# A hybrid Mamba and sparse-attention layer on one core: who loads the projection weights, and where the first norm's root is applied

## The chip, the cores and the metric

The kernel runs on one core of a Trainium2 chip. The metric is device time in microseconds, from runs without the profiler; three runs of the kernel before are given below, and the profiled execution has a time of its own. The core has a matrix engine (TensorE, "PE" in the profile; its weight loads are "PEld"), VectorE ("DVE"), ScalarE ("ACT"), GpSimd ("POOL") and SyncE ("SP"). SP issues most of the DMAs here, and POOL issues those that accumulate.

## The reference

One decoder layer on 512 tokens of width 1024, batch 1, in float32:

```
h    = rms_norm(x, norm1_g)
proj = h @ w_in                                  # 1024 x 5184
z, xbc, dt, q, kv, gates = split(proj)
y_ssm = ssd_mixer(z, xbc, dt, ...)               # conv of 4 taps, silu, 16 heads, 4 chunks of 128
y_nsa = rms_norm(nsa_mixer(q, kv, gates, ...), attn_norm_g)
x = x + concat([y_ssm, y_nsa]) @ w_out
h = rms_norm(x, norm2_g)
u = causal_dwconv(h @ ffn_w_up, ...)             # 1024 x 5632, 3 taps
x = x + (silu(ug) * uv) @ ffn_w_down
return rms_norm(x, final_norm_g)
```

`nsa_mixer` gives each query three attentions (over compressed blocks, selected blocks and a window); with 512 tokens all blocks are selected. Rotary embedding is applied to q and to the three kinds of k. The compressed keys and values come from blocks of 32 tokens through a small two-layer network. `rms_norm` divides each token's row by the root of its mean square: the root is one number per token, so it can be applied to `x` ahead of a product, or to the product behind it.

## The kernel before

**Exact products out of three fast ones.** A float32 operand is split into a high part (rounded to the fast format, `F32R`) and a low part (the rest). Each product is made of three matmuls: high by high, high by low, low by high. `hT` holds the two parts of the normed input, transposed: 8 blocks of 128 features by 512 tokens.

**Granules.** All big weights are cut into granules of 128 x 1024 numbers, 512 KB each, numbered in the order of their use: 0 to 39 are `w_in`, 40 to 55 `w_out`, from 56 the feed-forward weights. Of `w_in`, 0 to 3 are the two kinds of plain v, 4 and 5 the keys and 6 and 7 the values that get compressed, 8 and 9 further keys, 10 to 13 queries, 14 and 15 the first of xbc, and so on. Of `w_out`, 40 to 47 take the attention's output and 48 to 55 the SSM's. A granule comes into the chip in one of two ways:

- *split by the engines*: SP loads two halves `wr` of 256 KB, ACT or DVE rounds each to `wh`, and DVE or POOL subtracts to get `wl`;
- *split by loads* (granules `D0` to `D1 - 1`): POOL loads the whole granule to `wh` (the load rounds), ACT writes `-wh` into `wl` (1024 columns), and POOL loads the granule a second time, accumulating onto `wl`.

`wh` and `wl` have `N_WH` and `N_WL` buffers; halves `wr` and nearly all other tiles of 128 x 512 share `N_SLOT` slots. PSUM is a pool of 8 banks.

**Order.** The whole program is recorded first (`record`), with dependencies. Then `schedule` makes a list schedule from a table of costs: at each step it takes the operation that can start first, ties by priority, on five in-order engines, with limited buffers. Operations recorded with `DP` may go to DVE or POOL, plain copies to ACT or DVE. So any change of buffers, costs or operations shifts the order on every engine; the order that comes out is fixed at build time.

**The start** (`first_job`). `N_WARM` matmuls on zeros keep PE busy while the first loads come. Norm 1's root is not known yet, so the v products (`psa`, 96 matmuls) are made from `x` times the norm's gain, in temporary parts `xgh` and `xgl`, and the root is applied in `evac_v`. Beside this the sum of squares is made (`n1ss`), then its root (`n1r`, and `n1rb`: spread over all partitions). Then `hT` is made: per block one multiply by gain and root on DVE (`xT`), one copy to `hTh`, one subtract to `hTl`. After that come the products of granules 4 to 7 (`psb`, 24 matmuls each), and the small projection of dt and gates (`psd`, 16 matmuls).

**Compression.** The keys in `evac_c` are rotated (`rope`: four DMAs `rw` exchange halves, three operations on DVE or POOL), and then each pair is copied by four DMAs into `x2a` and `x2b`; `compress` gathers blocks from these into `cxb` and multiplies (`cps`). SP issues all of these DMAs.

**The middle** weaves attention (units of 128 queries, `pss`, `tb`, `o`) with the other projection granules. Then `ssd` (four chunks) is woven with `out_nsa`, the product of the attention's output with granules 40 to 47, and `out_ssm` follows with granules 48 to 55, four for each half of the columns: all four of a half are held while the four token tiles go by. The feed-forward is last, PE at work without a break.

Of the kernel before, what the change touches and what calls it, by code (L numbers as in the profile page):

```python
# [10 lines left out]
F32 = mybir.dt.float32  # L11
F32R = mybir.dt.float32r
# [7 lines left out]
P = 128  # L20
# [3 lines left out]
KC = 8  # L24
FF = 2816
NEG = -1.0e30
N_SLOT = 53
N_WH = 7
N_WL = 7
AHEAD = 3  # L30
LOOK = 2
D0, D1 = 8, 56
N_EAGER = 3
HEADS = (4, 2, 1, 1)
N_WARM = 10
P_MAX = 8
T_COLD = 6830.0
LAG = 3


# [128 lines left out]
class Program:  # L169
# [82 lines left out]
    def _cost(self, op, e, n, args, kw, ins, outs):  # L252
        is_ps = [v.buf.pool.tag == "b" for v in ins]
        if e == "PE":
            o, l = outs[0], ins[0]
            if l.buf.dt == BF16:
                return max(o.free / 2.4, 53 * l.free / 128) + 2.5, 0

            passes = 2 if l.buf.dt == F32 and n != "transpose" else 1
            cost = passes * max(o.free * passes / 2.4 + 13.3, 110 * l.free / 128)  # L260
            part = l.ids.shape[0]
            return cost + (190 if part <= 64 else 0), 0
        if e == "ACT":
            extra = sum(isinstance(kw.get(x), View) for x in ("scale", "bias", "accum_out"))
            return ins[0].free / 1.2 + (52 if is_ps[0] else 94) + 93 * extra, TABLE.get(args[2].name, 0)
        if n == "dma_start" and e == "POOL":
            v = outs[0]
            op.lat = v.ids.shape[0] * v.free * 4 / (180.0 if "accum_op" in kw else 360.0)
            return 1000.0, 0
        if e in ("DVE", "POOL"):  # L270
            f = max([v.free for v in ins] + [outs[0].free])
            if n == "reciprocal":
                cost = f * 6.25 + 70
            elif n == "memset":
                cost = f / 0.96 + 10
            elif n in ("tensor_scalar", "tensor_scalar_mul", "tensor_scalar_add", "tensor_scalar_max", "tensor_copy"):
                cost = f / (0.96 if is_ps[0] else 1.92) + 68 + 61 * (len(ins) > 1)
            else:
                cost = f / 0.96 + 75 + (61 if n == "scalar_tensor_tensor" and len(ins) > 2 else 0)
            if e == "DVE" and any(int(v.ids.flat[0]) // v.buf.row for v in ins + outs):  # L280

                cost += 97
            if f >= 64:
                big = [v for v in ins if v.free >= 64]
                sb = sum(v.buf.pool.tag != "b" for v in big)
                op.port[e] = e == "POOL" or sb > 1 or (sb == len(big) == 1 and not is_ps[0] and n not in ("reciprocal", "tensor_reduce"))
            return cost * (2.0 if e == "POOL" else 1.0), 0
        v = (outs + ins)[0]
        op.lat = v.ids.shape[0] * v.free * 4 / 360.0
        return 650.0, 0  # L290


# [119 lines left out]
def layer_kernel(ctx: ExitStack, tc: tile.TileContext, x, xt, win, wdtg, wout, wup, wdn, pack, gcol, rows, cw1, consts, rot, out):  # L412
# [17 lines left out]
    def slot(name, dt=F32, shape=(P, T)):  # L430
        return alloc(sp, shape, dt, name, "s", N_SLOT)

    def bank(name, shape=(P, T)):
        return alloc(pp, shape, F32, name, "b", 8)
# [300 lines left out]
    def job_dtg():  # L735
# [12 lines left out]
        raw64 = slot("dtg", F32, (64, T))  # L748
        S.activation(raw64, ps[64:128], AF.Copy)
        V.tensor_add(raw64, raw64, ps[0:64])  # L750
        yield 1.0
        tb = bank("dtgT", (P, NT, 64))
        for t in range(NT):
# [32 lines left out]
    def evac_c(which, pair):  # L786

        def f(ps):
            if which == "k":
                r = rope(ps, 1.0)  # L790
            else:
                r = slot("vcr")
                S.activation(r, ps, AF.Copy)
            x2 = slot("x2a"), slot("x2b")
            for a in range(2):
                own = slice(64 * a, 64 * a + 64)
                SP.dma_start(x2[a][0:64, :], r[own, :])
                SP.dma_start(x2[a][64:128, 0:511], r[own, 1:512])
            CX[which, pair] = x2
        return f  # L800
# [217 lines left out]

    def evac_xbc(i):
        def f(ps):  # L1020
            o = slot("xbc")
            w = [k("cw", 5 * i + j) for j in range(5)]
            S.activation(o, ps, AF.Identity, bias=w[4], scale=w[3])
            for d in range(1, 4):
                V.scalar_tensor_tensor(o[:, d:], ps[:, :T - d], w[3 - d], o[:, d:], op0=ALU.mult, op1=ALU.add)
            XB[i] = o
        return f

# [2 lines left out]
    def evac_z(qr):  # L1031
        def f(t, ps):
            if qr % 2 == 0:
                Z[t, qr // 2] = slot("z")
            S.activation(Z[t, qr // 2][:, (qr % 2) * 256:(qr % 2 + 1) * 256], ps, AF.Copy)
        return f

    SS = {}
# [159 lines left out]
    def nsa_root(h):  # L1198
        ps = bank("oss", (P, 2, 2))
        for t in range(2):  # L1200
            for p_ in range(2):
                mm(ps[:, t], ACC[h][:, p_, t], ones[:, 0:2], start=p_ == 0, stop=p_ == 1)
        r = rstd_of(ps[:, :, 0], 2, 1024, 1e-6, "nsa")
        for t in range(2):
            RS["nsa", 2 * h + t] = r[:, t:t + 1]


    def first_job():

        g0 = nxt(4)
        ps = [bank("psa") for _ in range(NT)]
        acc = slot("n1acc")
        for j in range(KC):
            g = gT[:, j:j + 1]
            xh, xl = slot("xgh", F32R), slot("xgl", F32R)
            S.activation(xh, xT[j], AF.Copy, scale=g)
            V.scalar_tensor_tensor(xl, xT[j], g, xh.bitcast(F32), op0=ALU.mult, op1=ALU.subtract)  # L1220
            if j % 2 == 0:
# [14 lines left out]
            mm(ss[:, t], acc[:, t * P:(t + 1) * P], ones[:, 0:2], start=True, stop=True)  # L1236
        r = rstd_of(ss[:, :, 0], NT, 1, 1e-6, "n1")
        RS["n1"] = r
        rb = bank("n1rb")
        for t in range(NT):  # L1240
            mm(rb[:, t * P:(t + 1) * P], r[:, t:t + 1].to_broadcast([P, P]), ident, start=True, stop=True)
        for j in range(KC):
            V.scalar_tensor_tensor(xT[j], xT[j], gT[:, j:j + 1], rb, op0=ALU.mult, op1=ALU.mult)
            S.activation(hT[0][:, j], xT[j], AF.Copy)
            DP.tensor_sub(hT[1][:, j], xT[j], hT[0][:, j].bitcast(F32))
        pr.first = False
        for t in range(NT):
            for z, ty in enumerate("sw"):
# [134 lines left out]
    def out_nsa(half):  # L1383
        if half == 0:
            for h in range(2):
                for g in range(4):
                    if g >= N_EAGER:
                        nsa_ops(g, h)
                nsa_root(h)
        for t in range(NT):  # L1390
            X1[t, half] = slot(f"xr{t}")
            SP.dma_start(X1[t, half], x[t * P:(t + 1) * P, half * 512:(half + 1) * 512])
        g0 = nxt(4)
        ws = [w_get(g0 + p_, 3 - p_) for p_ in range(4)]
        for t in range(NT):
            ps = bank(f"on{t}")
            for p_ in range(4):
                for j in range(2):
                    tri(ps, mix(t, 2 * p_ + j), [a[:, j * 512:(j + 1) * 512] for a in ws[p_]],
                        p_ == 0 and j == 0, p_ == 3 and j == 1)  # L1400
                yield 1.3
            V.scalar_tensor_tensor(X1[t, half], ps, RS["nsa", t], X1[t, half], op0=ALU.mult, op1=ALU.add)

    def out_ssm(half):
        g0 = nxt(4)
# [205 lines left out]
```

## Time and profile before

| | before |
|---|---|
| median of 3 runs | 919.08 us (918.53 to 921.29) |
| profiled execution, own time | 917.42 us |
| its span, first to last instruction | 915.6 us |
| PE busy | 883.9 us, 97% |
| DVE busy | 682.8 us, 75% |
| ACT busy | 433.0 us, 47% |
| mean granted TensorE clock | 0.994 |

The span is 1.8 us shorter than the profiled execution's own time; what lies outside is start and end. Busy time of PE is the time in which some matmul was in flight, and matmuls overlap, so it says where PE stood idle and not how fast it went. Where engines wait, the profile names what ended the wait.

### The profile page before, as it was taken

To read this page: it belongs to the slowest core of one execution; us is meant where nothing else is said; L and a number is where in the kernel's file an instruction comes from. 1 tells how busy PE (TensorE), PEld (TensorE's weight loads), DVE (VectorE), ACT (ScalarE), POOL (GpSimd) and SP (SyncE) were. 2 spreads that over 40 slices of the span, in tenths; PEclk is the share of its full clock that TensorE was granted. 3 is DMA by queue.
4 is the path that set the end of the run, shared out by engine and by line. 5 is a ranking of instruction groups with operands and counts; after the bars stand their busy time and mean duration, and the time that the engine had idled before them with its cause. 6 is when DMAs were issued, how large, how long until landed. Compare 5 with 4: busy or idle time off the path is not lost.

```text
span 915.6 us, 13236 instructions
## 1 busy us (share of the span) xinstructions
PE 883.9 (97%) x4621; PEld 727.6 (79%) x4621; DVE 682.8 (75%) x1466; ACT 433.0 (47%) x939; POOL 111.0 (12%) x138
## 2 busy tenths in 40 slices
PE   8998999999999999999999999999999999999996
PEld 5776777787887799888777779888888888888885
DVE  6956899998889876689898477777773347777535
ACT  5624577787676666578665244222321113222113
POOL 0331231111111111102322221000000000000000
PEclk9999999999999999999999999999999999999999
DMA  8798754454454454432859922111112661000002
GB/s 274 222 223 204 168 119 96 95 121 106 103 127 93 93 105 103 93 116 48 209 165 304 332 83 93 54 50 47 47 58 98 227 226 35 1 0 1 1 1 92
DMA packets 45217, 106.02 MB, mean 116 GB/s; under 512 B 5984, under 2 KB 6752, under 8 KB 45152
## 3 DMA queue, kind: packets, MB, share of 16 engines
q0 software_dynamic: 13824, 50.34, 24.6%
q1 hardware_dynamic: 31328, 54.86, 18.3%
q8 instruction: 36, 0.59, 0.3%
q14 instruction: 29, 0.24, 0.1%
HBM read 97.31 MB, written 2.10 MB: 109 GB/s over the span
## 4 chain that ended last, share of the span: by engine, by line
PE 74%; DVE 10%; DMA 6%; issue 6%; ACT 2%; POOL 2%; SPq 1%; POOLq 0%; DVEq 0%; ACTq 0%
PE psb L400 36%; PE dn L400 13%; PE psa L400 8%; PE pss L400 5%; PE tb L400 4%; PE o L400 4%; PE os L400 2%; DMA rw<-rx 1%; DMA x2b<-rx 1%; PE on L400 1%; DVE hTl L400 1%; DMA wl<-in_wout_dram 1%; DMA x2b<-vcr 1%; SPq L400 1%; DMA wr<-in_win_dram 1%
## 5 line engine op out<-in xcount | busy, mean ns | idle before, releaser
L400 PE MATMUL psb<-hTh,wh 128*128 128x512 f32 (+1 forms) x600 | 232.8, 390 | 2.5 <-ACT cup L400 1.0
L400 PE MATMUL psb<-hTl,wh 128*128 128x512 f32 (+1 forms) x600 | 230.4, 384 | 2.3 <-DVE hTl L400 2.3
L400 PE MATMUL psb<-hTh,wl 128*128 128x512 f32 (+1 forms) x600 | 230.0, 384 | 0.0
L400 ACT ACTIVATE wh<-wr 128x512 fp32r<-128x512 f32 x80 | 49.8, 631 | 202.0 <-PE psb L400 102.1
L400 PEld LDWEIGHTS psb<-hTh,wh 128*128 128x128 f32 x600 | 113.2, 189 | 23.7 <-ACT cup L400 1.5
L400 PEld LDWEIGHTS psb<-hTl,wh 128*128 128x128 f32 x600 | 113.3, 189 | 23.5 <-DVE hTl L400 3.6
L400 PEld LDWEIGHTS psb<-hTh,wl 128*128 128x128 f32 x600 | 113.2, 189 | 21.6
L400 DVE TENSOR_TENSOR wl<-wr,wh 128x512 fp32r<-128x512 f32 x133 | 90.2, 714 | 17.1 <-ACT wh L400 16.8
L400 DVE CAST wh<-wr 128x512 fp32r<-128x512 f32 x68 | 28.9, 426 | 91.9 <-PE psb L400 43.7
L400 ACT ACTIVATE p<-pss,nm 128x128 f32<-128x128 f32 (+3 forms) x128 | 66.8, 525 | 38.0 <-DVE nm L400 21.3
L400 PE MATMUL dn<-wh,gTh 128*128 128x512 f32 (+1 forms) x186 | 70.3, 378 | 0.0
L400 PE MATMUL dn<-wl,gTh 128*128 128x512 f32 (+1 forms) x186 | 70.3, 378 | 0.0
L400 PE MATMUL dn<-wh,gTl 128*128 128x512 f32 (+1 forms) x186 | 70.2, 378 | 0.0
L400 DVE TENSOR_TENSOR ptl<-tb,pth 128x512 fp32r<-128x512 f32 x80 | 54.3, 687 | 14.6 <-ACT pth L400 11.0
L400 ACT ACTIVATE wl<-wh 128x1024 fp32r<-128x1024 f32 x48 | 50.6, 1056 | 27.7 <-DMA wh<-in_wout_dram 14.9
L400 DVE TENSOR_REDUCE nm<-pss 128x1 f32<-128x384 f32 (+3 forms) x88 | 55.5, 633 | 4.0 <-PE pss L400 3.4
L400 PE MATMUL tb<-ck,p 128*128 128x128 f32 x320 | 51.4, 275 | 1.4 <-DVE p L400 1.0
L400 POOL TENSOR_TENSOR wl<-wr,wh 128x512 fp32r<-128x512 f32 x15 | 21.0, 1410 | 225.6 <-ACT wh L400 206.2
L400 ACT ACTIVATE pth<-tb 128x512 fp32r<-128x512 f32 x62 | 36.9, 598 | 21.9 <-PE tb L400 16.4
L400 POOL DMA_DIRECT2D wl<-in_win_dram x32 | 28.2, 882 | 150.4 <-ACT wl L400 136.3
L400 PEld LDWEIGHTS tb<-ck,p 128*128 128x128 f32 x320 | 37.5, 140 | 8.8 <-DVE p L400 1.2
L400 PEld LDWEIGHTS dn<-wh,gTh 128*128 128x128 f32 x186 | 35.0, 188 | 6.7 <-DVE xr L400 0.2
(325 smaller groups left out, 1739.2 us busy)
## 6 DMA issues: line engine op xcount, KB each, us to landing
wr<-in_wup_dram SPq DMA_DIRECT2D x88, 256.0 KB, 4.3
wh<-in_win_dram POOLq DMA_DIRECT2D x32, 512.0 KB, 4.1
wl<-in_win_dram POOLq DMA_DIRECT2D x32, 512.0 KB, 5.4
wr<-in_wdn_dram SPq DMA_DIRECT2D x44, 256.0 KB, 3.4
wh<-in_wout_dram POOLq DMA_DIRECT2D x16, 512.0 KB, 5.3
wl<-in_wout_dram POOLq DMA_DIRECT2D x16, 512.0 KB, 7.5
wr<-in_win_dram SPq DMA_DIRECT2D x16, 256.0 KB, 7.0
rw<-rx SPq DMA_DIRECT2D x56, 64.0 KB, 3.8
```

Source lines behind the costliest of these rows:

```text
L400: getattr(engines[op.eng], name)(*[real(a) for a in args], **{k: real(v) for k, v in kw.items()})
```

## The change

Four things change together:

1. Granules 8 to 15 and 48 to 55 are no longer split by loads but by the engines (`D0, D1` from 8, 56 to 16, 48). Five instead of seven buffers hold `wh` and `wl`, and the eight slots that fit in their place go to the common slots (53 to 61).
2. Norm 1's root is no longer multiplied into `hT`. `first_job` writes its parts `x` times gain straight into `hT`, and the later products are scaled where they are read: rope's `cos` and `sin` are multiplied by the root once, and xbc, the compressed values, dt and gates, and z get it at their reading from PSUM. For xbc this is a further DVE operation (`xu`) for each of 12 tiles.
3. `out_nsa` goes granule by granule over the four token tiles, with four PSUM banks open, instead of tile by tile with four granules held.
4. 14 instead of 10 warm-up matmuls, and other costs in the scheduler's table.

```diff
-N_SLOT = 53
-N_WH = 7
-N_WL = 7
+N_SLOT = 61
+N_WH = 5
+N_WL = 5
...
-D0, D1 = 8, 56
+D0, D1 = 16, 48
...
-N_WARM = 10
+N_WARM = 14
...
-T_COLD = 6830.0
+T_COLD = 5500.0
...
-            op.lat = v.ids.shape[0] * v.free * 4 / (180.0 if "accum_op" in kw else 360.0)
+            op.lat = v.ids.shape[0] * v.free * 4 / (145.0 if "accum_op" in kw else 290.0)
...
+        DP.tensor_mul(raw64, raw64, RS["rb"][0:64])
...
-                S.activation(r, ps, AF.Copy)
+                V.tensor_mul(r, ps, RS["rb"])
...
+            u = slot("xu")
+            V.tensor_mul(u, ps, RS["rb"])
...
-            S.activation(o, ps, AF.Identity, bias=w[4], scale=w[3])
+            S.activation(o, u, AF.Identity, bias=w[4], scale=w[3])
...
-            S.activation(Z[t, qr // 2][:, (qr % 2) * 256:(qr % 2 + 1) * 256], ps, AF.Copy)
+            S.activation(Z[t, qr // 2][:, (qr % 2) * 256:(qr % 2 + 1) * 256], ps, AF.Identity,
+                         scale=RS["n1"][:, t:t + 1])
...
-            xh, xl = slot("xgh", F32R), slot("xgl", F32R)
+            xh, xl = hT[0][:, j], hT[1][:, j]
...
-        for j in range(KC):
-            V.scalar_tensor_tensor(xT[j], xT[j], gT[:, j:j + 1], rb, op0=ALU.mult, op1=ALU.mult)
-            S.activation(hT[0][:, j], xT[j], AF.Copy)
-            DP.tensor_sub(hT[1][:, j], xT[j], hT[0][:, j].bitcast(F32))
+        rb = slot("rb")
+        S.activation(rb, pb, AF.Copy)
+        RS["rb"] = rb
+
+        for z in range(2):
+            DP.tensor_mul(cos_sin[z], cos_sin[z], rb)
...
+        ps = [bank(f"on{t}") for t in range(NT)]
+        g0 = nxt(4)
+        for p_ in range(4):
+            w = w_get(g0 + p_)
+            for t in range(NT):
+                for j in range(2):
+                    tri(ps[t], mix(t, 2 * p_ + j), [a[:, j * 512:(j + 1) * 512] for a in w],
+                        p_ == 0 and j == 0, p_ == 3 and j == 1)
+                yield 1.3
```

What this does to the order is seen at three places. First PE, right behind the v products `psa`. Before, granules 4 (`wh_316`), 5 (`wh_386`) and 6 (`wh_398`) start beside each other:

```order
L400 MATMUL psa<-wh_231,xgl 128x512 x4
L400 MATMUL psb<-hTh,wh_316 128x512
L400 MATMUL psb<-hTh,wh_386 128x512
L400 MATMUL psb<-hTh,wh_398 128x512
L400 MATMUL psb<-hTl,wh_316 128x512
L400 MATMUL psb<-hTh,wl_327 128x512
L400 MATMUL psb<-hTh,wh_316 128x512
L400 MATMUL psb<-hTl,wh_386 128x512
```

In the change, with `hT` already there, granule 4 (now `wh_331`) runs by itself to its end, and the others after it:

```order
L400 MATMUL psa<-wh_246,hTl 128x512 x2
L400 MATMUL n1rb<-ck,n1r 128x128 x4
L400 MATMUL psa<-wh_246,hTl 128x512 x2
L400 MATMUL psb<-hTh,wh_331 128x512
L400 MATMUL psb<-hTl,wh_331 128x512
```

What moved: nothing of `psb` stands beside another granule any more, and its first matmul no longer follows the making of `hT`.

Second SP, behind the loads of the compression's weights `cwv`. Before, the rotation's exchanges come next:

```order
L400 DMA cwv_340<-in_cw_dram 128x512
L400 DMA cwv_347<-in_cw_dram 128x512
L400 DMA rw<-rx 32x512 x8
L400 DMA x2a<-vcr 64x512
L400 DMA x2a<-vcr 64x511
```

In the change the halves of granules 8 to 14 stand ahead of them, and the copies of the rotated keys come before those of the values:

```order
L400 DMA cwv_317<-in_cw_dram 128x512
L400 DMA cwv_326<-in_cw_dram 128x512
L400 DMA wr<-in_win_dram 128x512 x14
L400 DMA rw<-rx 32x512 x8
L400 DMA x2a<-rx 64x512
```

What moved: 14 loads of 256 KB came onto the queue of the exchanges, and POOL's loads of these granules are gone.

Third DVE, ahead of the rotation of the first keys (`rw<-rw,sin`). In the change these rows stand there; `wh_471` is granule 7, `wh_487` 8, `wh_507` 9, `wh_538` 10 and `wh_576` 11:

```order
L400 TENSOR_TENSOR wl_483<-wr,wh_471 128x512
L400 TENSOR_TENSOR wl_499<-wr,wh_487 128x512 x2
L400 TENSOR_TENSOR wl_513<-wr,wh_507 128x512 x2
L400 CAST wh_538<-wr 128x512
L400 TENSOR_TENSOR wl_543<-wr,wh_538 128x512 x2
L400 CAST wh_576<-wr 128x512
L400 TENSOR_TENSOR wl_581<-wr,wh_576 128x512
L400 TENSOR_TENSOR rw<-rw,sin 128x512
```

What moved: before, only `COPY vcr<-psb` stands between the v evictions and this multiply; now the splits of granules 7 to 11 do, and that of granule 11 needs the `wh` buffer that granule 6 leaves.

## Rows read from the trace of the kernel before

**Rows 1.** The page: the span, and busy time of each engine

```profile
span 915.6 us, 13236 instructions
PE 883.9 (97%) x4621; PEld 727.6 (79%) x4621; DVE 682.8 (75%) x1466; ACT 433.0 (47%) x939; POOL 111.0 (12%) x138
```

**Rows 2.** Stretches: us, busy PE, PEld, DVE, ACT, POOL, clock, DMA share, GB/s

```profile
20.00:30.00 10.00, 9.96 (x48) 8.09 (x47) 9.09 (x26) 5.13 (x10) 1.71 (x2) 1.00 0.96 289
75.00:80.00 5.00, 2.89 (x18) 2.83 (x19) 2.35 (x16) 0.56 (x3) 0.00 (x0) 0.84 1.08 248
80.00:85.00 5.00, 4.01 (x14) 2.90 (x13) 3.30 (x14) 3.18 (x8) 0.55 (x1) 0.82 0.43 122
85.00:410.00 325.00, 319.96 (x1917) 262.64 (x1915) 277.82 (x624) 221.97 (x521) 52.24 (x69) 1.00 0.49 112
411.00:495.00 84.00, 80.51 (x490) 65.84 (x489) 79.85 (x181) 57.72 (x145) 22.43 (x30) 1.00 0.61 165
497.00:525.00 28.00, 26.24 (x116) 21.45 (x115) 13.62 (x30) 7.46 (x12) 5.96 (x6) 1.00 1.07 338
```

**Rows 3.** Waits of PE: line, what for, total us, times, longest

```profile
PE os L400 <- DMA wl<-in_wout_dram: 5.0, 2, 3.2
PE psb L400 <- DVE hTl L400: 2.3, 3, 1.2
PE psb L400 <- ACT cup L400: 1.0, 1, 1.0
```

**Rows 4.** Timeline of the start: first POOL's, ACT's, then PE's rows (start, us)

```profile
1.25 1.28 POOL L400 DMA_DIRECT2D wh<-in_win_dram  x2 [0.80 <-POOLq L1604]
3.87 0.63 ACT L400 ACTIVATE n1acc<-xT 128x512 f32<-128x512 f32 x1 [1.85 <-DMA xT<-in_xt_dram]
8.17 0.63 ACT L400 ACTIVATE wh<-wr 128x512 fp32r<-128x512 f32 x1 [3.66 <-DMA wr<-in_win_dram]
1.19 4.45 PE L400 MATMUL warm<-zero 128*128 128x512 bf16 x10 [1.19 <-DVE zero L400]
8.85 2.08 PE L400 MATMUL psa<-wh,xgh 128*128 128x512 f32 x4 [3.21 <-ACT wh L400]
13.85 1.09 PE L400 MATMUL psa<-wh,xgh 128*128 128x512 f32 x4
48.40 0.50 PE L400 MATMUL psb<-hTl,wh 128*128 128x512 f32 x1 [1.23 <-DVE hTl L400]
63.74 0.39 PE L400 MATMUL psb<-hTh,wh 128*128 128x512 f32 x1
```

**Rows 5.** Timeline of SP's queue: exchanges and copies of the compression

```profile
28.09 3.31 SPq L400 DMA_DIRECT2D cwv<-in_cw_dram  x2
49.84 5.04 SPq L400 DMA_DIRECT2D rw<-rx  x8
69.80 1.10 SPq L400 DMA_DIRECT2D x2b<-rx  x2
```

**Rows 6.** Timeline of PE at the compression

```profile
77.11 2.64 PE L400 MATMUL cps<-cxb,cwk 128*128 128x130 f32 x16 [3.08 <-issue]
```

**Rows 7.** Timeline of PE in the SSM's half of the output projection

```profile
523.73 0.39 PE L400 MATMUL os<-wh,hTh 128*128 128x512 f32 x1
525.09 0.39 PE L400 MATMUL os<-wh,hTh 128*128 128x512 f32 x1
528.73 0.65 PE L400 MATMUL os<-wl,hTh 128*128 128x512 f32 x1 [3.25 <-DMA wl<-in_wout_dram]
532.17 0.48 PE L400 MATMUL os<-wl,hTh 128*128 128x512 f32 x1
```

**Rows 8.** Groups of DVE's instructions: xcount, busy us, mean ns, idle before

```profile
L400 DVE TENSOR_TENSOR wl<-wr,wh 128x512 fp32r<-128x512 f32 x133 | 90.2, 714 | 17.1 <-ACT wh L400 16.8 <-DMA wr<-in_wdn_dram 0.3
L400 DVE TENSOR_TENSOR ptl<-tb,pth 128x512 fp32r<-128x512 f32 x80 | 54.3, 687 | 14.6 <-ACT pth L400 11.0 <-PE o L400 2.3 <-PE tb L400 0.5
```

**Rows 9.** DMA issues: xcount, KB each, median us from issue to landing

```profile
rw<-rx SPq DMA_DIRECT2D x56, 64.0 KB, 3.8
```

More of the change, by code (lines that the diff above doesn't have):

```diff
@@ L288, in _cost @@
         v = (outs + ins)[0]
-        op.lat = v.ids.shape[0] * v.free * 4 / 360.0
+        op.lat = v.ids.shape[0] * v.free * 4 / 290.0
         return 650.0, 0
@@ L1020, in f @@
         def f(ps):
+            u = slot("xu")
+            V.tensor_mul(u, ps, RS["rb"])
             o = slot("xbc")
             w = [k("cw", 5 * i + j) for j in range(5)]
-            S.activation(o, ps, AF.Identity, bias=w[4], scale=w[3])
+            S.activation(o, u, AF.Identity, bias=w[4], scale=w[3])
             for d in range(1, 4):
-                V.scalar_tensor_tensor(o[:, d:], ps[:, :T - d], w[3 - d], o[:, d:], op0=ALU.mult, op1=ALU.add)
+                V.scalar_tensor_tensor(o[:, d:], u[:, :T - d], w[3 - d], o[:, d:], op0=ALU.mult, op1=ALU.add)
             XB[i] = o
@@ L1238, in first_job @@
         RS["n1"] = r
-        rb = bank("n1rb")
+        pb = bank("n1rb")
         for t in range(NT):
-            mm(rb[:, t * P:(t + 1) * P], r[:, t:t + 1].to_broadcast([P, P]), ident, start=True, stop=True)
-        for j in range(KC):
-            V.scalar_tensor_tensor(xT[j], xT[j], gT[:, j:j + 1], rb, op0=ALU.mult, op1=ALU.mult)
-            S.activation(hT[0][:, j], xT[j], AF.Copy)
-            DP.tensor_sub(hT[1][:, j], xT[j], hT[0][:, j].bitcast(F32))
+            mm(pb[:, t * P:(t + 1) * P], r[:, t:t + 1].to_broadcast([P, P]), ident, start=True, stop=True)
+        rb = slot("rb")
[3 more added lines that the diff above has]
+            DP.tensor_mul(cos_sin[z], cos_sin[z], rb)
         pr.first = False
@@ L1392, in out_nsa @@
             SP.dma_start(X1[t, half], x[t * P:(t + 1) * P, half * 512:(half + 1) * 512])
-        g0 = nxt(4)
-        ws = [w_get(g0 + p_, 3 - p_) for p_ in range(4)]
         for t in range(NT):
[L1396 to L1402, printed above, removed]
+            V.scalar_tensor_tensor(X1[t, half], ps[t], RS["nsa", t], X1[t, half], op0=ALU.mult, op1=ALU.add)
     def out_ssm(half):
```

## The prediction

> **What bounds the kernel now.** I read the page first: PE is busy 97% of the span [rows 1]. PE's work is the same matmuls before and after, but for four warm-ups, so what can be won or lost is what PE loses: idle time, and time at the lower clock. I therefore went on to PE's waits, summed by what ended them: 5.0 us for the low parts of granules 48 to 55, 2.3 us for `hTl`, 1.0 us behind the compression [rows 3]. The timeline then gives each one its place and what it costs beyond the idle time itself.
>
> The start [rows 4]: ten warm-ups end at 5.64, PE stands 3.21 us for the first `wh`, and begins at 8.85. The first twelve matmuls take until 13.85, where twelve at full speed take 2.72: their pitch is 0.227 us, from six steps in 1.36 us at 523.73 to 525.09 [rows 7]. ACT could not round the first half before it landed, at 8.17, 4.3 us behind the first block of x (3.87), and POOL had issued two whole granules, 1 MB, from 1.25 on [rows 4]. The stretch from 20 to 30 moves 289 GB/s at a share of 0.96 [rows 2], so 256 KB take 0.9 us and 1 MB 3.6.
>
> The compression: PE waits 3.08 us [rows 6], and has 0.84 and 0.82 of its clock in the two stretches of five microseconds from 75 on [rows 2]. SP had issued the exchanges and copies from 49.84 to 70.9 (69.80 + 1.10) [rows 5], while the DMA engines were full (share 1.08) [rows 2]. In `out_ssm` the share is 1.07 [rows 2]; PE waits 3.25 us for a low part, and its next eight matmuls, from 528.73 to 532.17, take 0.43 each [rows 7].
>
> In the other two stretches it is DVE to look at. From 85 to 410 it is busy 277.8 of 325 us, with PE at 320. From 411 to 495, where `ssd` and `out_nsa` are woven, it is busy 79.9 of 84: there DVE sets the pace as much as PE does [rows 2].
>
> **The start, -4.3.** Without POOL's two granules the first half should land about 0.9 us behind the block of x, at 4.8. With ACT's 0.63 it is ready at 5.5. PE is then still in its warm-ups: ten take 4.45 us [rows 4], so fourteen reach 7.2, or 6.4 if the last four run at the high clock. I take the first matmul at 6.8. For the clock I have one row: matmuls without a break from 8.85 were at full speed by 13.85 [rows 4]. The warm-ups begin at 1.19 and the products now follow with no gap, so by that row the clock is up at about 6.2, and the twelve matmuls take 2.72: they end at 9.5 and not at 13.85. Bounds: -5.0 if the warm-ups end at 6.4 and nothing else is late; -2.0 if the first half lands no earlier and only the clock is gained.
>
> The Trainium skill, "DMA: Bandwidth & Descriptors", section "Queues, rings and completion order", says that each DMA engine takes turns between the queues that have work. By that rule POOL's queue takes only as much as SP's own, the half would have landed 0.9 us earlier and not 3.6, the first matmul would start at 8.0 and the term would be -3.1; the row with its 4.3 us between two SP loads [rows 4] bears out more than a fair turn.
>
> **Norm 1, -2.8.** The three waits for `hTl` are 2.3 us [rows 3]; the matmul behind each starts a further 0.1 to 0.2 late, as the 0.50 in place of 0.40 shows [rows 4, 7]. With `hT` written by the first job nothing remains to wait for. Its replacement, two multiplies of `cos` and `sin` on DVE at 0.69 each [rows 8], stands ahead of the first rotation only. Bounds -2.3 and -3.7. What follows is late on no queue: the weights of granules 4 to 7 are loaded and split as before. So the small projection's end, at 63.74 [rows 4], moves by 7.1 to about 56.6.
>
> **The compression, -4.0.** PE now reaches `cps` ten matmuls behind that point, at 58.9. The keys' path: granule 11's buffer comes free when granule 6 is done, at about 47.5; DVE splits it and then does the six operations of both rotations and one eviction, at some 0.6 each (0.69 with their overlap) [rows 8], until about 53. The second pair's copies need four DMA issues (0.55 to 0.63 each in the rows of this queue [rows 5]) and the landing, 3.8 by the exchanges' median [rows 9]: about 60, with the gathering 60.5 to 61. So a wait of about 2 us is left of the old loss of 6.0: 3.1 of waiting [rows 6], 1.0 behind the products [rows 3], 1.7 for a clock that was short by 0.16 and 0.18 of five microseconds [rows 2], and 0.2 for the restarts. Bounds 0 and -6.0. The cover is that no weights move then: POOL's two loads per granule, which filled the engines from 50 to 80, are gone.
>
> **The output projection's second half, -6.0.** The waits for DMA, 5.0 [rows 3], end, since these low parts are now made on chip, and with the second wait goes the cold stretch, eight matmuls at 0.43 in place of 0.227, 1.6 us [rows 7]: 6.6 together. What is new: 16 subtractions at 0.71 and as many roundings. DVE is busy 13.6 of 28 us there [rows 2], so 11 us fit. With five buffers a half's second granule waits for the first one of the half before; that one ends 12 + 12 matmuls ahead of the switch, 5.4 us, and a split takes about 2.5. I leave 0.6 for the first switch, where a split stands behind an eviction on DVE. Bounds -3 and -6.6.
>
> **What DVE gets.** Twelve `xu` at 0.69 (nearest row: `ptl`, which also reads PSUM [rows 8]) and one of the compressed values, 9 us in the stretch from 85 to 410, where 47 are free [rows 2]. Between 0 (all in the gaps) and +9 (all on the path), nearer to the first by the 85%: +1.5. In the woven stretch, three of the new subtractions stand ahead of the last chunk, 2.1 us on an engine that is 95% busy; POOL takes over about as much: +0.5, bounds -1 and +5. The banks are a rival. The scale of z and the extra multiply of gates lie under ACT (222 of 325) and DVE in the same stretch. The feed-forward is left as it is.
>
> **The sum** against the profiled execution's 917.4 (span 915.6 and 1.8 around it): -4.3 - 2.8 - 4.0 - 6.0 + 1.5 + 0.5 = -15.1, so 902.3. The median of the runs is 1.7 above the profiled execution: 904.
>
> **Rivals.**
>
> *The keys wait on SP's queue.* The 14 halves stand ahead of the exchanges. By 0.9 us each behind `cwv`, issued until 31.4 [rows 5], they are through at 44, before DVE wants the exchanges at 48. If they crawl at half that rate, being held by slots, they end at 56.6, everything behind moves by 8 us, PE waits as long and loses its clock as at 77 [rows 6]: the term turns from -4.0 to about +3, and the time is 911. For it: one queue in order. Against: 61 slots, and nothing else that moves. Chance 0.17. The page and section named above say that within one queue the engines take descriptors in the order of the ring, which is this rival's mechanism; no row here has loads ahead of an exchange to show it.
>
> *The banks.* `on` now holds four of eight PSUM banks through the woven stretch, and each of the four chunks takes some 17 others in turn (1 `cb`, 2 `xst`, 4 `seg`, 2 each of `yd`, `yo`, `bt`, `stt`, 2 `tb`), 68 in all, evicted by a DVE that is 95% busy. If each costs PE 0.22 us more, the 15.1 are used up; at 0.3 us the stretch is 20 us longer, and the time 924, slower than before. Against: 192 `on` matmuls, 43 us of work that needs no new bank, lie between to fill. Chance 0.06.
>
> *The head is not won.* The change gets rid of the load for norm 1 but the first job does not run earlier, since the splits at the start wait as before (the first half at 8.17): -2 in place of -7.1 there, and the compression keeps its loss of 6.0 (PE comes late, but so do the keys). 904 + 5 + 4 = 913, faster by 0.6%. Chance 0.1.
>
> *More is won.* All terms at their lower bounds: -5.0 - 3.7 - 6.0 - 6.6 + 0 - 1 = -22.3, 7 below the forecast, and 897. If half of the 5 us that PE stands idle between 85 and 410 [rows 2] goes with the weights that no longer move there, 894. Chance 0.1.
>
> **Numbers.** The forecast, 899 to 909, has 0.55; the queue and the head 0.27, more 0.1, the banks 0.06, the rest unknown. The range takes in all but the banks: 894 to 914. A change of 0.3% (2.8 us, about what a measurement can tell here) is passed by all cases but the banks and mixtures: faster 0.90, same 0.04, slower 0.06.
>
> **What would show it.** Right: PE's first product near 7 with a pitch of 0.23 from there; no `hTl` among PE's waits; the small projection done near 57; no `os` wait for DMA, and no stretch below a clock of 1 after 60. Wrong: `cps` waiting 3 us or more, `rw` issued after 50; gaps ahead of `seg`, `yd` or `xst` between 400 and 480; DVE idle less than 3% and PE below 95% there.

## The result, and the profile after

| | before | after |
|---|---|---|
| median of the runs | 918.81 us (4 runs, 917.98 to 921.29) | 911.17 us (4 runs, 910.11 to 911.45) |
| profiled execution, own time | 917.42 us | 911.45 us |
| its span | 915.6 us | 909.6 us |

The ratio is 0.991, with a 95% interval of 0.989 to 0.9931: faster by 0.9%, 7.6 us. The forecast was 904, twice the gain; the time lies outside the narrow forecast (899 to 909) and inside the wide range (894 to 914).

First the page and the stretches of [rows 1, 2], for the changed kernel (us, then busy PE, PEld, DVE, ACT, POOL, clock, DMA share, GB/s):

```profile
span 909.6 us, 13307 instructions
...
PE 887.3 (98%) x4625; PEld 724.3 (80%) x4625; DVE 694.9 (76%) x1475; ACT 434.7 (48%) x966; POOL 93.6 (10%) x110
```

```profile
75.00:80.00 5.00, 5.00 (x25) 3.91 (x24) 3.80 (x10) 2.81 (x6) 0.00 (x0) 1.00 0.51 150
80.00:85.00 5.00, 5.00 (x29) 4.22 (x28) 4.64 (x11) 4.49 (x9) 0.00 (x0) 1.00 0.22 52
85.00:410.00 325.00, 318.90 (x1917) 262.74 (x1917) 280.38 (x636) 227.62 (x542) 51.47 (x67) 0.99 0.47 107
411.00:495.00 84.00, 78.68 (x466) 63.84 (x465) 80.35 (x169) 52.93 (x138) 29.49 (x30) 1.00 0.69 202
497.00:525.00 28.00, 28.00 (x126) 22.57 (x125) 18.09 (x44) 8.46 (x19) 0.00 (x0) 1.00 0.41 147
```

The span is 6.0 us shorter and yet PE is busy 3.4 us longer than in [rows 1], with the same matmuls and four short warm-ups. That is the first sign that something made the matmuls themselves longer. The two stretches from 75 to 85, where the compression stood before, are full and at clock 1, where [rows 2] had 2.89 and 4.01 us of five; the compression's first products now stand at 61, and that stretch is full too:

```profile
60.00:65.00 5.00, 5.00 (x30) 3.95 (x29) 3.76 (x12) 2.98 (x13) 0.00 (x0) 1.00 0.89 204
```

`out_ssm` is full as well. The stretch with a clock under 1 is now the one from 85 to 410.

The largest waits of PE, in place of [rows 3]:

```profile
PE tb L400 <- ACT p L400: 3.5, 2, 3.0
PE os L400 <- DVE t L400: 2.4, 1, 2.4
PE warm L400 <- DVE zero L400: 1.2, 1, 1.2
PE psa L400 <- ACT wh L400: 1.1, 1, 1.1
```

All three waits of [rows 3] are gone. New are 3.5 us for `p`, attention's weights, and 2.4 us for `t` at the first matmul of `out_ssm`.

The timeline of the start, and of the places of [rows 4, 6] (ACT's row first, then PE's):

```profile
4.86 0.63 ACT L400 ACTIVATE wh<-wr 128x512 fp32r<-128x512 f32 x1 [0.41 <-DMA wr<-in_win_dram]
```

```profile
1.19 4.63 PE L400 MATMUL warm<-zero 128*128 128x512 bf16 x14 [1.19 <-DVE zero L400]
5.55 1.30 PE L400 MATMUL psa<-wh,hTh 128*128 128x512 f32 x4
6.69 1.09 PE L400 MATMUL psa<-wl,hTh 128*128 128x512 f32 x4
...
58.58 0.39 PE L400 MATMUL psd<-hTl,wd 128*128 128x512 f32 x1
...
61.28 0.49 PE L400 MATMUL cps<-cxb,cwk 128*128 128x130 f32 x2
```

The first product comes at 5.55 instead of 8.85, the small projection's last matmul at 58.58, and `cps` at 61.28 has no wait ahead of it. The exchanges of the keys, issued from 49.84 in [rows 5], now go from 39.87.

How far the changed kernel is ahead of the one before at matmuls that both have (start of the row in one trace less start in the other, us), with the forecast's terms added up to the same place. The third column is a run of the experiments below, in which `hT` stands where it should:

| PE's matmul | after | after, `hT` in place | forecast |
|---|---|---|---|
| first `psb` (35.10 before) | 3.2 | 4.2 | 4.3 |
| first one behind `psd` (63.74) | 4.9 | 6.4 | 7.1 |
| first z product (314.42) | 8.7 | 11.3 | 9.6 |
| first `on` (402.70) | 9.3 | 11.7 | 9.6 |
| first `os` (491.96) | 8.4 | 10.7 | 9.1 |
| first of the feed-forward (545.52) | 13.0 | 16.2 | 15.1 |
| first `dn` (679.22) | 9.5 | 15.8 | 15.1 |
| end of the span | 6.0 | 15.5 | 15.1 |

Up to the feed-forward the changed kernel is 13.0 us ahead. Then it loses 7.0 us in a part of the program that the change does not touch, and in which PE waits once, for 0.75 us. ACT reads each finished granule of the feed-forward once, so its rows give the pace: `ug` comes every second granule, 48 matmuls of 512 columns. Before:

```profile
609.01 0.76 ACT L400 ACTIVATE ug<-psb,pk 128x512 f32<-128x512 f32 x1
...
619.89 0.76 ACT L400 ACTIVATE ug<-psb,pk 128x512 f32<-128x512 f32 x1
```

and after:

```profile
608.60 0.77 ACT L400 ACTIVATE ug<-psb,pk 128x512 f32<-128x512 f32 x1
...
619.80 0.77 ACT L400 ACTIVATE ug<-psb,pk 128x512 f32<-128x512 f32 x1
```

10.88 us against 11.20: 226.7 ns a matmul against 233.3, at a granted clock of 1 in both. Of the matmuls of 512 columns, those that read `hT` are slower; `dn`, which multiplies other tiles by the same kind of weights, has a median step of 227 ns in both traces. `os` and `psa` of 512 columns that read `hT` mostly step by 232 to 235 ns too.

The second loss is at the start of attention. PE's rows there, and POOL's:

```profile
105.14 0.23 PE L400 MATMUL pss<-cmask,idb 128*128 128x128 bf16 x1
108.32 1.21 PE L400 MATMUL tb<-ck,p 128*128 128x128 f32 x4 [2.96 <-ACT p L400]
110.22 0.79 PE L400 MATMUL o<-pth,vs 128*128 128x512 f32 x1 [0.69 <-ACT pth L400]
111.54 0.48 PE L400 MATMUL tb<-ck,p 128*128 128x128 f32 x1 [0.53 <-ACT p L400]
111.67 0.78 PE L400 MATMUL psb<-hTh,wh 128*128 128x512 f32 x1
```

```profile
86.82 0.56 POOL L400 DMA_DIRECT2D wh<-in_win_dram  x1 [12.91 <-issue]
87.38 0.94 POOL L400 DMA_DIRECT2D wl<-in_win_dram  x1
```

PE waits 2.96, 0.69 and 0.53 us, and its matmuls behind that are twice as long; the stretch from 110 to 115 has a clock of 0.50. The `psb` product before this one ended at 100: from there to 111.67 PE has nothing in its order but attention's chain (queries, `pss`, exp, `tb`). The queries' exchange is issued from 87.16, and beside POOL's two loads it takes 5.3 to 7.0 us to land.

### The profile page after: what moved, and what is told of

The parts are those of the page before. It is cut to its first block, busy times and chain, and to the rows that moved or that the text cites. A ratio compares the mean times of both kernels' runs of the same rounds, so it can differ in the third digit from the quotient of the medians.

```text
span 909.6 us, 13307 instructions
## 1 busy us (share of the span) xinstructions
PE 887.3 (98%) x4625; PEld 724.3 (80%) x4625; DVE 694.9 (76%) x1475; ACT 434.7 (48%) x966; POOL 93.6 (10%) x110
## 4 chain that ended last, share of the span: by engine, by line
PE 86%; DVE 9%; ACT 2%; issue 2%; DMA 1%; SPq 0%; DVEq 0%; ACTq 0%
PE psb L400 41%; PE dn L400 13%; PE psa L400 7%; PE tb L400 5%; PE pss L400 5%; PE os L400 5%; PE o L400 4%; PE on L400 2%; PE yd L400 1%; DVE xsd L400 1%; DMA xT<-in_xt_dram 1%; DVE wl L400 1%; DVE xr L400 1%; ACT p L400 0%; PE cs L400 0%
## 5 line engine op out<-in xcount | busy, mean ns | idle before, releaser
L400 PE MATMUL psb<-hTh,wh 128*128 128x512 f32 (+1 forms) x600 | 236.3, 395 | 0.0
L400 PE MATMUL psb<-hTh,wl 128*128 128x512 f32 (+1 forms) x600 | 232.9, 388 | 0.0
L400 PE MATMUL psb<-hTl,wh 128*128 128x512 f32 (+1 forms) x600 | 232.8, 388 | 0.0
L400 ACT ACTIVATE wh<-wr 128x512 fp32r<-128x512 f32 x110 | 67.4, 632 | 228.0 <-PE psb L400 130.0
L400 DVE TENSOR_TENSOR wl<-wr,wh 128x512 fp32r<-128x512 f32 x166 | 112.1, 709 | 14.8 <-ACT wh L400 14.5
L400 ACT ACTIVATE p<-pss,nm 128x128 f32<-128x128 f32 (+3 forms) x128 | 66.8, 526 | 37.3 <-DVE nm L400 22.3
L400 PEld LDWEIGHTS dn<-wh,gTl 128*128 128x128 f32 x186 | 35.0, 188 | 6.6
L400 PEld LDWEIGHTS dn<-wl,gTh 128*128 128x128 f32 x186 | 35.0, 188 | 6.4
```

What stands on the lines that cost most here:

```text
L400: getattr(engines[op.eng], name)(*[real(a) for a in args], **{k: real(v) for k, v in kw.items()})
```

## The experiments

All ratios are to the kernel before, run beside them on the same chip (915 to 921 us).

**Where `hT` stands.** In the built programs `hTh` starts at byte 22144 of each partition before, a multiple of 64, and at 17056 after, 32 beyond one: buffers get their place in the order of first use, and `hT`, now used ahead of the constants `ck`, comes behind the 32 bytes of `gT` and the 512 of `ones`. `hTl` lies 16384 bytes further each time.

```diff
-    hT = (const("hTh", (P, KC, T), F32R), const("hTl", (P, KC, T), F32R))
-    gT = const("gT", (P, KC))
-    SP.dma_start(gT, gcol)
+    hT = (const("hTh", (P, KC, T), F32R),
+          const("hTl", (P, KC * T + 8), F32R)[:, :KC * T].rearrange("p (j t) -> p j t", j=KC))
+    gT = const("gT", (P, KC + 8))
+    SP.dma_start(gT[:, :KC], gcol)
```

> The changed kernel with 32 bytes of padding ahead of hT (and 32 behind it, so that no buffer after hT moves by anything but 64); the order of instructions on every engine is the same. In the changed kernel each 512-column matmul that reads hT starts 233 to 234 ns after the one before it, where the kernel before had 227, and those that don't read it have 227 in both. Theory: it is hT's place in SBUF, which the change moved from a multiple of 64 bytes to 32 beyond one. Then 227 comes back: some 1,056 products of the feed-forward at 6.5 ns are 6.9 us, and about 950 earlier ones up to 4 to 5 more where PE sets the pace: 900 to 904. Rival: the slower pitch comes from something else that the change did to hT or to the weights' buffers (five pairs at other addresses, or who writes hT); then 233 stays and the time is 911.

Measured: 902.15 us, ratio 0.9829 [0.9804, 0.9855].

The control has `KC + 16` numbers for `gT` and none behind `hT`, so that `hTh` is at 17120:

> The control: 64 bytes of padding ahead of hT, so that it stands again 32 beyond a multiple of 64, and everything else stands where it does in the run with 32 bytes. Theory of the address: 233 to 234 ns, 911. If any new distance between hT and the other buffers is enough, 227 and 900 to 904.

Measured: 910.56 us, 0.9921 [0.99, 0.9942].

The reverse widens, in the kernel before, the 64 bytes of `sel` to 96 and pads behind `hT`: `hTh` goes from 22144 to 22176.

> The reverse: the kernel before with hT moved by 32 bytes and nothing else (same order on every engine; the buffers behind hT move by 64). Theory of the address: its products go from 227 to 233 ns, and the time rises by 7 to 12 us, to 926 to 931. Rival (the changed kernel's buffers or writers of hT): no change, 918.8.

Measured: 924.99 us, 1.0077 [1.0056, 1.0098]. The pace of the feed-forward, first in the changed kernel with 32 bytes more, then in its control with 64, then in the kernel before with `hT` moved:

```profile
604.12 0.76 ACT L400 ACTIVATE ug<-psb,pk 128x512 f32<-128x512 f32 x1
...
615.00 0.76 ACT L400 ACTIVATE ug<-psb,pk 128x512 f32<-128x512 f32 x1
```

```profile
607.27 0.76 ACT L400 ACTIVATE ug<-psb,pk 128x512 f32<-128x512 f32 x1
...
618.47 0.76 ACT L400 ACTIVATE ug<-psb,pk 128x512 f32<-128x512 f32 x1
```

```profile
600.22 0.77 ACT L400 ACTIVATE ug<-psb,pk 128x512 f32<-128x512 f32 x1
...
611.42 0.76 ACT L400 ACTIVATE ug<-psb,pk 128x512 f32<-128x512 f32 x1
```

10.88, 11.20 and 11.20 us: the pace follows the place, in both kernels, with the same order of instructions. The control, whose buffers behind `hT` stand exactly where they do in the first run, keeps the slow pace. So the place of `hT` costs the change 8.4 us (910.56 less 902.15), and the rival (other weights' buffers, another writer of `hT`) falls. What inside the chip makes it so, no run here shows.

**The wait at the start of attention.** All of these are made on the run with `hT` in place (902.15 us; it waits 3.0 us for `p` at 104 and has a clock of 0.61 and 0.71 from 105 to 115). The first one splits four more granules on chip:

```diff
-D0, D1 = 16, 48
+D0, D1 = 20, 48
```

> The run with hT in place, and granules 16 to 19 split on chip as well (split by loads from 20 on). It is for the new wait: in the changed kernel PE stands 2.96 us for p at 105, 0.69 and 0.53 behind it, and then has half its clock for 6.8 us. Theory of the loads: POOL's two loads for granules 16 and 17, 1 MB, are issued at 86.8 and 87.4, together with the exchange of the second pair of queries of group 0 (87.2 to 89.9), which lands 5.3 to 6.9 us after its issue where 2.6 is the median; with those loads put off the exchange lands in 3 us, the wait is under 1, the clock stays up, and the time is 5 us below the run with hT in place. Rival: DVE is what is late, with the splits of granules 14 and 15 ahead of the queries' last steps; four more granules to split make it later, the wait is 3 us or more, and the time is that of the run with hT in place or above it.

Measured: 902.31 us (898.87 to 905.41), 0.9827 [0.9799, 0.9856]. The exchange of those queries lands after 2.0 us, the longest wait for `p` is 0.9, and the clock is 1 from 100 to 125. As much is lost elsewhere: six halves `wr` (two without the edit) now stand ahead of a key's exchange on SP's own queue, that exchange takes 5.5 us from issue to landing in place of 2.1, DVE waits for it, and PE waits for the compressed keys with its clock down:

```profile
PE cps L400 <- DVE kch L400: 2.5, 1, 2.5
```

```profile
60.00:85.00 25.00, 22.33 (x106) 17.81 (x105) 20.07 (x64) 13.40 (x36) 0.00 (x0) 0.93 0.53 143
```

The theory of the loads holds for the exchange and for the wait, and misses the time.

The other direction:

```diff
-D0, D1 = 16, 48
+D0, D1 = 12, 48
```

> The run with hT in place, with granules 12 to 15 split by loads as well. It takes eight subtractions of 0.69 from DVE and eight roundings from ACT between 70 and 100, and puts some 4 MB more on the DMA engines. Theory of the loads: the exchanges of keys and queries run beside more loads and land later (5 us and over), the wait for p is 3 us or more, the clock falls at the compression too, 903 to 906. Rival (DVE is what makes the start of attention late): queries and p come 2 to 4 us sooner, the wait is under 1.5 us, the clock stays up, 897 to 899.

Measured: 901.95 us, 0.9831 [0.9808, 0.9855]. Both expectations miss (and the loads added are 2 MB, not 4, since SP's halves go). The exchange takes 6.3 us, as the loads would have it, but the wait is 2.5 and no longer than in the run without; DVE's relief is not seen in the time either. Fewer or more granules split on chip do not bring the time down; one wait is traded for another.

Now the loads alone are put off, until the exchange has landed:

```diff
-    def rope(ps, scale):
+    def rope(ps, scale, pool=False):
...
-        DP.tensor_mul(w, w, cos_sin[1])
+        m = (PD if pool else DP).tensor_mul(w, w, cos_sin[1])
+        if pool:
+            QX.append(m)
...
-            PD.dma_start(wh[i], arr[j // 2, :, j % 2])
+            d = PD.dma_start(wh[i], arr[j // 2, :, j % 2])
+            if QX and i == 17:
+                pr.order(QX[0], [d])
...
-        r = rope(ps, 0.125)
+        r = rope(ps, 0.125, (g, half) == (0, 1))
```

(and the same for the load added for granule 16; `QX` is a list that starts empty).

> The run with hT in place, and the two loads on POOL's queue that ran beside the second exchange of group 0's queries are put behind it: POOL itself multiplies this exchange by sin, and the load of granule 17 and the one added for granule 16 are ordered behind that. Theory of the loads: the exchange, 5.5 to 7.0 us from issue to landing in the run with hT in place, lands in 2.0; the queries are ready 3 to 4 us earlier, PE's wait of 3 us for p at 104 falls under 1, and the half clock of 6.8 us behind it goes: -4 to -6 us, 896 to 898. Rival: the queries are late through DVE, whatever the exchange does; then the wait stays at 2 us or more and the time at 902. Second rival: the loads come late for granules 16 and 17 and PE waits for them; the wait moves and the time stays.

Measured: 901.25 us, 0.9813 [0.9792, 0.9834]. Issue to landing of that exchange, first with the loads beside it, then with the loads put off (KB, median us):

```profile
rw<-rx SPq DMA_DIRECT2D x4, 64.0 KB, 6.4
```

```profile
rw<-rx SPq DMA_DIRECT2D x4, 64.0 KB, 2.0
```

So the loads made this exchange late by 4.4 us, and the 3 us of waiting at 104 went with them. But PE's next waits grew:

```profile
113.45 0.70 PE L400 MATMUL tb<-ck,p 128*128 128x128 f32 x4 [0.18 <-DVE p L400]
115.43 0.70 PE L400 MATMUL tb<-ck,p 128*128 128x128 f32 x4 [1.28 <-DVE p L400]
...
116.82 0.50 PE L400 MATMUL o<-pth,vs 128*128 128x512 f32 x1 [0.26 <-ACT pth L400]
117.77 0.79 PE L400 MATMUL o<-ptl,vs 128*128 128x512 f32 x1 [0.46 <-DVE ptl L400]
```

The clock fell there instead (0.86 from 100 to 125, as without). Removing what was late first showed what was late next.

Is it the wait that costs, or the clock behind it? Thirteen matmuls that compute nothing fill PE's gap:

```diff
-                mm(ps[:, i], idb, cmask[:, None, :].to_broadcast([P, 2, P]), start=False, stop=True)
+                SM[0] = mm(ps[:, i], idb, cmask[:, None, :].to_broadcast([P, 2, P]), start=False, stop=True)
...
+        if (u["g"], u["qt"], u["ty"]) == (0, 0, "s"):
+            pr.order(SM[0], [mm(tb, idb, cmask[:, None, :].to_broadcast([P, 4, P]), start=True, stop=True)
+                             for _ in range(13)])
```

> The run with hT in place, with thirteen matmuls that compute nothing (mask by identity, 512 columns each, into the bank that the first transposes overwrite) put into PE's order ahead of the wait for p at 104. They take 13 x 0.22 = 2.9 us, the length of the wait. Theory: the wait's 3 us are lost as before, but PE's clock, which was granted at half for 6.8 us behind it, stays up: half of 6.8 is given back, -3.4 us, 898.5 to 899. Rivals: the clock falls all the same, and the time stays at 902 (the gaps of 0.7 and 0.5 behind the wait are enough), or the thirteen matmuls push the attention's chain back by their own length: 902 to 905.

Measured: 900.94 us, 0.982 [0.9796, 0.9844]. They took 2.97 us as meant, and the wait behind them is gone. The two gaps that follow, 0.69 and 0.81, stayed, and the clock fell behind these, from 110 on. The stretch from 105 to 115 without the filling, and with it:

```profile
105.00:110.00 5.00, 2.15 (x5) 1.02 (x5) 4.88 (x10) 3.64 (x10) 3.76 (x3) 0.61 0.58 105
110.00:115.00 5.00, 4.95 (x18) 3.95 (x19) 5.00 (x13) 4.02 (x14) 1.40 (x1) 0.71 0.01 3
```

```profile
105.00:110.00 5.00, 3.35 (x19) 2.06 (x18) 4.88 (x12) 3.65 (x11) 3.75 (x3) 1.00 0.62 105
110.00:115.00 5.00, 5.00 (x18) 4.00 (x17) 5.00 (x13) 3.71 (x13) 1.40 (x1) 0.66 0.00 0
```

Half of the slow time is given back, 1.7 us of the clock's 3.4; the median is 1.2 us lower. The profiled execution gains 0.7 us between the first matmul behind `psd` and the first z product, so not all of the 1.7 arrives. The first rival was nearer than the theory.

Last, PE gets other work to do there. `yield 8.0` at the start of attention's stream puts the products 8 us ahead of attention in the program's order, more than one granule:

```diff
         gen, tail = None, None
+        yield 8.0
         while ti < len(units):
```

With the loads put off as well:

> The run with the exchange ahead of the loads, and the products put ahead of attention by 8 us of the weaving's own count, so that PE's order has more products left where attention starts. In that run PE's wait of 3 us at 104 was gone, but 4 us of smaller waits came at 112 to 116 and the clock fell there for 6.8 us. Theory: what is short at the start of attention is work for PE that doesn't hang on the chain of queries, exps and transposes; with a product more in reserve the waits there fall to 1 to 2 us in all, the clock stays up, and the time is 896 to 898. Rival: DVE, busy 24.6 of 25 us from 95 to 120 in that run, sets the time there whatever PE has to do; the waits come back elsewhere in the stretch, and the time stays at 901.

Measured: 895.56 us (895.52 to 896.74), 0.9764 [0.974, 0.9788].

```profile
100.00:125.00 25.00, 23.33 (x126) 18.61 (x125) 24.24 (x58) 16.99 (x54) 3.42 (x5) 1.00 0.57 134
```

This is the same stretch of the run with `hT` in place:

```profile
100.00:125.00 25.00, 20.97 (x115) 16.49 (x114) 23.32 (x55) 16.37 (x48) 9.60 (x8) 0.86 0.30 76
```

PE stood idle for 4.0 us there and lost 3.5 to the clock (0.14 x 25); now it is idle for 1.7 and at clock 1. These 5.9 us are most of the 6.3 by which the span is shorter (893.8 for 900.1). DVE is as busy as ever (24.2 of 25 us): the rival that DVE sets the time there falls. And with the loads left where they are:

> The run with hT in place, with the products put ahead of attention by 8 us of the weaving's own count, and the loads on POOL's queue left where they are: the fourth of four (neither 902.2, the loads put off alone 901.3, both 895.6). If work for PE in reserve is all that was short at the start of attention, it gives 896 to 897 and the clock stays up, though the queries' exchange lands after 5 to 7 us as before. If the exchange's delay must go as well, PE still waits 1.5 us and more there, the clock falls, and the time is 899 to 902.

Measured: 898.63 us, 0.9782 [0.9762, 0.9802]; PE still waits 1.2, 0.7 and 0.5 us and has a clock of 0.93 from 100 to 125. This is the stretch:

```profile
100.00:125.00 25.00, 22.50 (x110) 17.12 (x110) 22.48 (x55) 17.38 (x51) 3.87 (x5) 0.93 0.43 96
```

Of the four, neither is 902.2, the loads alone give 0.9, the products alone 3.5, both together 6.6. They ran on four chips, on which the kernel before has medians of 917.4 to 918.9, so a difference of 1 us between them is not clear of the noise: by the ratios the gains are 1.5, 4.3 and 6.0. The products are the larger part by either count. In the traces it is the order that leaves PE without other work, and with the products ahead the clock still falls beside the late exchange and no longer falls without it; of each there is one trace.

**The parts alone.** Norm 1's part on the kernel before, with `hT` in place, and then the other part:

```diff
-N_SLOT = 61
-N_WH = 5
-N_WL = 5
+N_SLOT = 53
+N_WH = 7
+N_WL = 7
...
-D0, D1 = 16, 48
+D0, D1 = 8, 56
```

(against the run with `hT` in place; loads' costs and `out_nsa` as before too)

> Norm 1's part of the change alone (hT written by the first job and in place on a multiple of 64, the root applied behind the products, 14 warm-ups); granules 8 to 55 split by loads, buffers, costs and output projection as before. By the terms of the forecast: norm 1 -2.8, of the start the clock's 2.0 alone, since POOL's two granules still run beside the first loads, +1.5 for DVE: -3.3 of the kernel before, 914. If the compression's or the output's loss goes with it, 908 or less; if the multiplies behind the products cost what lies open between 85 and 410, 919 or more.

Measured: 927.17 us (924.81 to 938.29), 1.0117 [1.0078, 1.0157]: slower than before, 13 us from the 914 expected. PE's waits between 100 and 145, and two stretches:

```profile
PE tb L400 <- ACT p L400: 4.4, 2, 3.6
PE tb L400 <- DVE p L400: 2.2, 1, 2.2
```

```profile
100.00:125.00 25.00, 19.15 (x100) 15.26 (x100) 22.73 (x46) 12.96 (x40) 8.23 (x9) 0.81 0.67 141
125.00:140.00 15.00, 13.65 (x58) 10.99 (x59) 12.03 (x30) 6.73 (x20) 1.34 (x2) 0.75 0.05 10
```

It is the start of attention again, more than twice as deep: 6.6 us of waits, and clocks that are short by 0.19 x 25 + 0.25 x 15 = 8.5 us. At the first `tb` the kernel is 1.4 us ahead of the one before (119.39), at the first `on` 11.0 behind (413.73). Most of it is this one place. What the multiplies behind the products cost is not told apart.

> The other part alone: granules 16 to 47 split by loads, 61 slots and five pairs of buffers, the planner's loads at 290, the output projection granule by granule; norm 1 as before, ten warm-ups, hT where the kernel before has it. By the terms: start -3 (the first half lands earlier, the warm-ups end sooner), compression -4.0, output -6.0, woven +0.5: -12 to -13, 905. Theory of the new wait (loads against exchanges at the start of attention): 3 us or more of PE waiting for p show here too, with the clock at half, and it is 908 to 910. The parts alone should add up to the run with hT in place, -15.

This kernel is the one before with the lines above the other way round, and the changed `out_nsa`. Measured: 907.97 us, 0.9887 [0.9866, 0.9908]; 3.3 us of waiting for `p` and a clock of 0.86 from 100 to 125, as the theory of the new wait had it. The parts alone give +8.4 and -10.8 (medians beside 918.77), together -2.4 and not -15. Over half of the 13 us that are missing are lost ahead of attention. At the first matmul behind `psd` the run with `hT` in place is 6.4 us ahead of the kernel before (the table above), norm 1's part alone is 0.6 behind (64.32), and the other part alone 0.8 behind (64.53). In the latter PE has its first product 3.0 us sooner (5.84) and then waits for the making of `hT`, with a clock of 0.75 from 30 to 36 and 0.72 from 42 to 48:

```profile
PE psb L400 <- ACT hTh L400: 2.8, 1, 2.8
PE psb L400 <- DVE hTl L400: 2.2, 2, 1.5
```

So the early start alone is lost again at the making of `hT`. In norm 1's part the first product comes as late as before (9.17), and behind it PE waits 1.8 and 1.4 us for DVE (`vw`, `vcr`), more than the 2.3 that were to be won; why those waits are gone in the whole change is not told apart. Behind that place each kernel has its own order at the start of attention, norm 1's part with much the deeper loss.

Last, the changed kernel with `hT` in place and `out_nsa` as before:

> The run with hT in place, with the output projection's first half as it was before (four granules held, one bank at a time, xr loaded ahead). My forecast has the new order cost nothing in itself and the woven stretch lose 0.5 us to the subtractions; theory: the new order is what lets a granule go after a quarter of the half, so that with five pairs of buffers the old one makes PE wait for the second half's granules, 3 to 5 us, 905 to 907. Rival (the banks): the four banks held by the new order are what costs, and the old order is faster, 899 to 901.

Measured: 905.32 us (903.63 to 907.27), 0.9861 [0.9838, 0.9884]. The new order is worth some 3 us, as expected, though the intervals of the two ratios overlap; the rival's faster old order is not borne out. But no wait for a granule is in the trace; `ssd` waits for DVE in small pieces (`sg` 1.6, `xsd` 1.1, `yg` 0.8, `xdh` 0.8). What makes them is not settled.

## Why the prediction came out as it did

**The direction and the wide range held; the step that failed is "The feed-forward is left as it is".** I took it that matmuls with the same operands keep their pitch, and put 0.227 us for each. The change moves the buffer that they read, and each matmul of 512 columns on `hT` takes 6.6 ns more: 6.3 us of the feed-forward (it loses 7.0 us as built and 0.7 with `hT` in place) and 8.4 in the median. No row of before could show it, but the order of first use, which sets the buffers' places, could have been read from the change. With `hT` in place the profiled span is 15.5 us shorter, where the sum said 15.1, and the median is 902.2, where the forecast was 904.

**What was luck.** The wide range held because it takes in rivals that did not come about: 911 is the time that *the keys wait on SP's queue* had, and no key waited. That the sum agrees with the run in place is in part luck too. With the loads put off and the products ahead, the first `os` comes 18.1 us ahead instead of 10.7, so the middle had some 7 us more to give than it gave: a gain that I did not see was used up by a loss that I did not see.

**The terms, with `hT` in place** (the table above): the start 4.2 for 4.3. Norm 1 gave 2.2 for 2.8. From there to the woven stretch 5.3 came for the 2.5 of the compression's 4.0 and DVE's 1.5; the new wait at the start of attention is inside this. The woven stretch lost 1.0 for 0.5, and the output projection gave 5.5 for 6.0. Each is within its bounds, except norm 1, which misses them by 0.1; the compression and DVE's part can't be told apart, since the new order mixes their stretches.

**The start.** The first half is rounded at 4.86, 3.3 us earlier than in [rows 4], as the rows of before had it: POOL's two granules were what it waited for. The parts alone show it, for in both SP's queue starts with the same loads in the same order. With POOL's two granules beside them (norm 1's part) and without (the other part):

```profile
8.49 0.63 ACT L400 ACTIVATE wh<-wr 128x512 fp32r<-128x512 f32 x1 [3.85 <-DMA wr<-in_win_dram]
```

```profile
5.16 0.63 ACT L400 ACTIVATE wh<-wr 128x512 fp32r<-128x512 f32 x1 [0.43 <-DMA wr<-in_win_dram]
```

The Trainium skill ("DMA: Bandwidth & Descriptors", section "Queues, rings and completion order") states that a DMA engine takes turns between the queues, a packet at a time. My estimate of 0.9 made equal bytes of these turns, which the page does not say; the trace decides for 3.3. The queries' exchange points the same way: 256 KB beside POOL's 1 MB land in 6.4 us and without those loads in 2.0. The first product's 6.8 was a guess at the clock: behind the same warm-ups, the eight from 3.73 on take 2.10 us in the changed kernel's trace and 3.57 in that with `hT` in place, and the first product comes at 5.55 and 6.79. Two small figures of the sum do not come out of its rows, and neither moves it: fourteen warm-ups at 0.445 reach 7.4 and not 7.2, and the lower bound, 13.85 less 9.12, is -4.7 and not -5.0.

**The compression and the keys' rival.** `cps` waits nowhere and the exchanges go at 39.87, so the wait of 2 us that the sum left there was not paid, and the rival *keys wait on SP's queue* did not come about in the change. (The share of 1.08 that I set beside the exchanges is that of 75 to 80; from 50 to 75 it is 0.90 to 1.10, so the reading stands.) Its mechanism was there to be had: with four more granules split on chip, loads ahead of a later exchange on SP's queue brought a wait of 2.5 us to a later `cps`. The same section of the Trainium skill says that the engines take descriptors of one queue in the ring's order; the exchange of 5.5 us behind six loads agrees.

**What I did not see** is that the planner's new order can empty PE's queue of products where attention starts. The sum puts this at nothing, and the sign that I gave, no stretch below a clock of 1 after 60, failed there. I looked at DVE's free time as a mean over 325 us, and the stretch that mattered is 25 us long, with DVE busy for 22.2 of them and PE's next product behind the transposes. The rival *banks* did not come about, and neither did *more is won*. With 32 bytes, loads put off and another order at one place the kernel comes to 895.6, a span 21.9 us shorter; that this is near that rival's 22.3 says nothing for it, since the time was won by other edits than its bounds.

## What to carry to other kernels

When a change adds, drops or reorders buffers, look where the operands of the bulk of the matmuls come to lie; here a multiple of 64 bytes was better than 32 beyond one for 512 columns, and no other distance was tried. A slower pace with no wait and a full clock is the sign. Where instructions are ordered by a plan, compare PE's queue around the first unit of a dependent chain, and keep independent products in reserve there. Measure the parts of a change alone, but don't add them up: here +8 and -11 made -15, since the early start without the early `hT` was lost again, and each order had its own loss at attention.

## What was not expected of the hardware

- Matmuls of 512 columns on `hT` step by 226.7 ns with `hTh` at byte 22144 or 17088 of the partition, and by 233.3 at 17056, 17120 and 22176 (32 beyond a multiple of 64). It is so whether `hT` streams (`psb`) or is the loaded side (`os`, `psa`). Matmuls of 256 columns go the other way, by less: the z products step by a median of 120 ns in place and 117 to 118 out of place.
- A 256 KB exchange on SP's queue lands in 2.0 us when POOL's loads are put off and in 6.4 beside 1 MB of them.
